# Moving the decay tables of a delta rule from the opening gates of a mixer to its inverse

## The chip, the cores and the metric

The kernel runs on one core of one Trainium2 chip. The metric is the device time of one execution in microseconds, the median of several runs; smaller is better. The core has a matrix engine (TensorE, in the rows PE for products and PEld for loading their weights), two engines that do most of the elementwise work (VectorE, DVE, and ScalarE, ACT), GpSimd (POOL), and queues that start transfers (mainly SP's). Each engine works through its own instructions in the order in which they were written out for it, and waits on semaphores for the others.

## What is computed

The reference is a first block (a mixer and a mixture of experts), followed by a second block of two layers. Each layer is a mixer of three branches and a feed-forward network. The change lies in the first branch of the mixer, a gated delta rule over chunks of 64 places:

```python
g = -jnp.exp(a_log) * jax.nn.softplus(a + dt_bias)
G = jnp.cumsum(gate_chunks(g), axis=-1)
decay = jnp.exp(jnp.where(causal, G[..., :, None] - G[..., None, :], -jnp.inf))
kk = jnp.einsum('bhnck,bhnsk->bhncs', k, k)
M = jnp.where(strict, beta[..., :, None] * kk * decay, 0.0)
T = lax.linalg.triangular_solve(eye + M, ...)          # the inverse
qk = jnp.einsum('bhnck,bhnsk->bhncs', q, k) * decay
q_dec = q * jnp.exp(G)[..., None]
g_last = jnp.exp(G[..., -1])
```

The other two branches are a sparse attention and a gated recurrence (HGRN). Queries, keys and values of the delta rule go through a short convolution and a SiLU first. There are 256 tokens, 1024 channels and 4 heads of 128.

## The kernel before

Everything is in float32; a dense projection is made exact enough by splitting both operands into a high and a low part and adding three products. `dense` (L193) does one 1024 by 256 projection: it loads the weights, and for each half of them `split` (L173) makes the high part `whi` with a cast on ScalarE and the low part `wlo` with a subtraction on VectorE; TensorE then does 24 products per half, 48 in all, into one PSUM bank. There are two buffers each of `whi` and `wlo`, so the cast for a half has to wait until TensorE is through with the half two before it. The bank is one of two that all dense projections of a mixer take turns with, and it comes free when the projection has been read out of it.

A mixer (L1458) opens with the step "gates": small projections, the gates of the delta rule (`delta_gates`, L1568), and the first part of the HGRN gates ("cf"). In `delta_gates` the running sums G of the decays are made, and from them the two tables of 128 by 512 per token half t: `E`, the exponential of minus the distance between two places' sums (four Abs activations that read a PSUM bank with a bias per head, and one Exp), and `eG`, the exponential of the sum itself. `dgl` is the last column of each chunk. On ScalarE these are 4 + 1 + 1 activations per token half and two small copies. `E` is first read in `delta_inverse` (L1645, making `N`), and `eG` near the end of the branch.

Then come the steps in the order of `emit` (L1181): k0 and k1 (the two halves of the key projection), qi, bq, sp0, ci, inv, v1, and so on. k0 and k1 are read out by `conv` (L1445): per block of 128 channels a scaled copy on ScalarE (L1449), in the second block also a copy `raw` (L1452), and three multiply-adds on VectorE (L1456); `silu2` follows (L1560). The step "inv" forms the keys' Gram matrix, `N`, and a blockwise inverse in six levels. "hg" is the HGRN.

What stands when on each engine is set by a list scheduler at build time: each step has a priority from its place in `order` (L1180), where an earlier place is more urgent among the instructions that the scheduler holds to be ready ("gates" is place 0, "inv" comes after both key halves, qi, bq, sp0 and ci); `issue_after(x)` keeps an instruction behind x on its engine. The same code runs for both layers, so the program has two mixers of this kind; in the trace before, the first opens at about 867 us and the second at about 1288 us.

Of the kernel before, what the change touches and what calls it, by code (L numbers as in the profile page):

```python
# [13 lines left out]
AF = mybir.ActivationFunctionType  # L14
# [3 lines left out]
P = 128  # L18
# [46 lines left out]
class K:  # L65
# [106 lines left out]

    def split(self, hi, lo, src):  # L173

        self.nc.scalar.copy(hi, src)  # L175
        with self.tc.issue_after(self.normed0) if self.normed0 else contextlib.nullcontext():
            self.nc.vector.tensor_sub(lo, src, hi.bitcast(F32))  # L177

# [1279 lines left out]
    def mixer(self, l, mp, hh, hl, hu, rb):  # L1458
        nc, v = self.nc, self.v2[l]
# [6 lines left out]
        T = lambda name, shape, dt=F32, tag=None, bufs=1: mp.tile([P, *shape], dt, name=name, tag=tag or name, bufs=bufs)  # L1466
# [18 lines left out]
        with self.level("gates"):  # L1485
            self.dense32(wb(), wv, [(2312, P), (2696, 68), (2048, 8)], hu, ev, blocks=((0, P), (P, 76)))

            ps = self.bk("delta")
# [8 lines left out]
            ps = self.bk("delta")  # L1497
# [5 lines left out]
            gt = self.delta_gates(T, v, baN)  # L1503
# [9 lines left out]
        qkv = [T("dqkv", (4, S), tag="d4", bufs=N_D4) for _ in range(3)]  # L1513

        def load(n, u):
            def ev(a):
                for b in range(2):
                    c = 2 * u + b
                    self.conv(qkv[n][:, c, :], a[:, b, :],
                              [v["conv"][:, k, 4 * n + c:4 * n + c + 1] for k in range(4)],  # L1520
                              T("raw", (S,), bufs=2) if b else None)
                x = qkv[n][:, 2 * u:2 * u + 2, :]
                self.silu2(T, x, x)
            self.dense(wv, [(512 * n + 256 * u, 256)], X, ev)
        oh, ol = (self.big(n, other) for n in ("oh", "ol"))
        sz, sg = T("sz", (2, 512)), T("sg", (2, S))
        qi, bq, cq, ci = (T(n, (2, S)) for n in ("qi", "bq", "cq", "ci"))
        dn = {}

        def z(n):  # L1530
            self.dense(wv, [(1536 + 256 * n, 256)], X,
                       lambda a: self.silu2(T, sz[:, :, n * S:(n + 1) * S], a), tokens=True)
        steps = dict(
            k=lambda n: load(1, n), v=lambda n: load(2, n), q=lambda n: load(0, n), z=z,
            inv=lambda: dn.update(self.delta_inverse(T, qkv[1], gt)),
            rest=lambda: self.delta_rest(T, qkv, gt, dn),
            chunks=lambda: self.delta_chunks(T, v, dn, sz, oh, ol),

# [29 lines left out]
    def delta_gates(self, T, v, baN):  # L1568
        nc, V = self.nc, self.nc.vector
        hv = lambda a: a.rearrange("p (h c) -> p h c", h=4)  # L1570
        bt, ga, gb = T("bt", (2, 4)), T("ga", (2, 4)), T("gb", (2, 4))
        V.tensor_tensor(ga, baN[:, :, 4:], v["dt"][:, None, :].to_broadcast([P, 2, 4]), op=OP.add)
        nc.scalar.activation(gb, ga, AF.Abs)
        with self.tc.issue_after(self.gelu) if self.gelu else contextlib.nullcontext():
            self.table = nc.scalar.preload_act_table_set("natural_log_exp_and_others").ins
            with self.tc.issue_after(self.table):
                nc.scalar.activation(gb, gb, AF.Exp, scale=-1.0)
        nc.scalar.activation(gb, gb, AF.Ln, bias=1.0)
        V.scalar_tensor_tensor(ga, ga, 0.0, gb, op0=OP.max, op1=OP.add)
        V.scalar_tensor_tensor(ga, ga, -1.0, v["a"][:, None, :].to_broadcast([P, 2, 4]), op0=OP.mult, op1=OP.mult)  # L1580
        nc.scalar.activation(bt, baN[:, :, :4], AF.Exp, scale=-1.0)
        V.tensor_scalar(bt, bt, 1.0, None, op0=OP.add)
        V.reciprocal(bt, bt)

        ps = self.bk("delta")
        g2 = ga.rearrange("p t h -> p (t h)")
        nc.tensor.matmul(ps[:, :8], self.c("tri"), g2, start=True, stop=True, skip_group_check=True)
        nc.tensor.matmul(ps[:, 8:16], self.c("bones"), g2, start=True, stop=True, skip_group_check=True)
        G, nG, eg, ed = T("G", (8,)), T("nG", (8,)), T("eg", (2, 4)), T("ed", (2, 4))
        V.tensor_copy(G, ps[:, :8])  # L1590
        V.tensor_scalar(nG, G, -1.0, None, op0=OP.mult)
        nc.scalar.activation(eg.rearrange("p t h -> p (t h)"), ps[:, :8], AF.Exp)
        V.tensor_tensor(ed.rearrange("p t h -> p (t h)"), ps[:, 8:16], G, op=OP.subtract)
        nc.scalar.activation(ed, ed, AF.Exp)

        eG, E = T("eG", (2, 4, P), tag="d4", bufs=N_D4), T("E", (2, 4, P), tag="d4", bufs=N_D4)
        for t in range(2):
            ps = self.bk("delta")
            for h in range(4):
                nc.tensor.matmul(ps[:, h * P:(h + 1) * P], ga[:, t, h:h + 1].to_broadcast([P, P]), self.c("tri"),  # L1600
                                 start=True, stop=True, skip_group_check=True)
            for h in range(4):
                k = 4 * t + h
                nc.scalar.activation(E[:, t, h, :], ps[:, h * P:(h + 1) * P], AF.Abs, bias=nG[:, k:k + 1])
            nc.scalar.activation(E[:, t], E[:, t], AF.Exp, scale=-1.0)
            nc.scalar.activation(eG[:, t], hv(ps), AF.Exp)
        gl = T("dgl", (4, 4))
        for t in range(2):
            nc.scalar.copy(gl[:, 2 * t:2 * t + 2, :], eG[:, t, :, 63:P:64].rearrange("p h n -> p n h"))
        return dict(bt=bt, eg=eg, ed=ed, eG=eG, E=E, gl=gl)  # L1610

    def sumsq(self, T, x):

# [383 lines left out]
```

## Time and profile before

| | |
|---|---|
| time, median of 3 runs | 1686.42 us (1682.34 to 1689.22) |
| the profiled execution, its own time | 1691.02 us |
| its span, first to last instruction | 1689.2 us |
| TensorE busy | 1615.7 us, 96% |
| VectorE busy | 919.5 us, 54% |
| ScalarE busy | 639.2 us, 38% |
| mean granted TensorE clock | 0.983 of full |

The profile's page gives shares over the whole span. What a change in one place does is read from the timeline and the waits of that place: which engine ended a wait of TensorE there, and what that engine was doing just before. A granted clock of 1.00 is the level of 2.4 GHz, 0.50 that of 1.2 GHz; a mean between them over a stretch tells how much of it was spent at each.

### The profile page before, as it was taken

How to read it: one execution, taken by the hardware profiler on the slowest of the kernel's cores; microseconds unless marked ns; L12 is line 12 of the kernel's file. 1: busy time of each engine (PE TensorE's matmuls, PEld its weight loads, DVE VectorE, ACT ScalarE, POOL GpSimd, SP SyncE). 2: the span in 40 equal slices, each digit the busy share in tenths (PEclk: the TensorE clock that was granted, in tenths of full speed). 3: DMA queues.
4: the chain of work that ended last, by engine and by line, in shares of the span. 5: the costliest groups of instructions: out<-in, count | busy, mean ns of one | idle time of the engine just before them, and what ended most of it. 6: DMA issues, size and time to landing. Idle time of an engine off the chain costs nothing.

```text
span 1689.2 us, 25550 instructions
## 1 busy us (share of the span) xinstructions
PE 1615.7 (96%) x10391; PEld 1218.3 (72%) x10391; DVE 919.5 (54%) x1873; ACT 639.2 (38%) x1102; POOL 21.8 (1%) x54
## 2 busy tenths in 40 slices
PE   6999999998999999999989999899999999989997
PEld 4778788973444344333478888799988988789986
DVE  2665445661212121121275597778847779778865
ACT  3543233441111011011164353455645545355643
POOL 1000000200000000000000000000000000000000
PEclk9999999998999999999998999999999999999999
DMA  8634545896999999999932142455762322435553
GB/s 310 212 107 127 198 152 161 267 397 272 421 420 421 421 420 420 421 420 421 378 112 75 32 144 76 150 174 178 231 212 64 106 65 90 150 114 192 181 188 137
DMA packets 162201, 381.72 MB, mean 226 GB/s; under 512 B 14180, under 2 KB 123308, under 8 KB 135200
## 3 DMA queue, kind: packets, MB, share of 16 engines
q1 hardware_dynamic: 160640, 378.45, 60.9%
q8 instruction: 83, 1.36, 0.3%
q0 software_dynamic: 1008, 1.33, 0.3%
q14 instruction: 38, 0.31, 0.1%
q10 hardware_dynamic: 432, 0.27, 0.1%
HBM read 378.98 MB, written 1.05 MB: 225 GB/s over the span
## 4 chain that ended last, share of the span: by engine, by line
PE 63%; DVE 7%; ACT 4%; DMA 2%; issue 1%; DVEq 0%; ACTq 0%
PE bk L186 56%; DVE wlo L177 1%; DMA w<-in_ffn_w_down 1%; ACT whi L175 1%; PE bk L1326 1%; PE bk L1666 1%; PE bk L1679 1%; PE bk L1677 1%; PE bk L1078 1%; ACT pscr L151 1%; DMA mw<-in_moe_w 1%; DVE xg L1273 0%; PE bk L1620 0%; DVE x L1266 0%; PE bk L1283 0%
## 5 line engine op out<-in xcount | busy, mean ns | idle before, releaser
L177 DVE TENSOR_TENSOR wlo<-w,whi 128x1024 fp32r<-128x1024 f32 x236 | 287.7, 1222 | 197.2 <-ACT whi L175 186.8
L175 ACT CAST whi<-w 128x1024 fp32r<-128x1024 f32 x236 | 246.2, 1048 | 298.7 <-PE bk L186 264.1
L186 PE MATMUL bk<-hh,whi 128*128 128x256 f32 x960 | 277.2, 289 | 14.8 <-ACT whi L175 8.1
L186 PE MATMUL bk<-hh,wlo 128*128 128x256 f32 x960 | 277.2, 289 | 6.7 <-DVE wlo L177 6.7
L186 PE MATMUL bk<-hl,whi 128*128 128x256 f32 x960 | 275.3, 287 | 0.0
L186 PEld LDWEIGHTS bk<-hh,whi 128*128 128x128 f32 x960 | 187.8, 196 | 17.8 <-ACT whi L175 9.0
L186 PEld LDWEIGHTS bk<-hh,wlo 128*128 128x128 f32 x960 | 187.9, 196 | 9.4 <-DVE wlo L177 8.1
L186 PEld LDWEIGHTS bk<-hl,whi 128*128 128x128 f32 x960 | 187.7, 196 | 0.4
L186 PE MATMUL bk<-w,xg 128*64 128x512 f32 x584 | 156.1, 594 | 2.8 <-ACT xg L1045 2.8
L1068 DVE TENSOR_TENSOR whi<-whi,bk 128x512 f32<-128x512 f32 x16 | 11.0, 687 | 237.9 <-PE bk L186 210.5
L186 PEld LDWEIGHTS bk<-w,xg 128*64 128x64 f32 x584 | 49.3, 137 | 87.6 <-issue 83.2
L186 PE MATMUL bk<-mw,xg 128*64 128x512 f32 x376 | 99.5, 594 | 1.5 <-ACT xg L1045 1.5
L186 PE MATMUL bk<-w,whi 128*64 128x512 f32 x296 | 95.5, 598 | 0.0
L1456 DVE SCALAR_TENSOR_TENSOR cv<-bk,fc,cv 128x255 f32<-128x255 f32 (+1 forms) x160 | 76.6, 479 | 2.8
L186 PEld LDWEIGHTS bk<-mw,xg 128*64 128x64 f32 x376 | 31.7, 137 | 52.4 <-issue 48.9
L186 PE MATMUL bk<-ah,whi 128*128 128x256 f32 x224 | 65.0, 290 | 2.6 <-ACT whi L175 2.6
L186 PE MATMUL bk<-whi,ah 128*128 128x256 f32 x224 | 64.1, 288 | 0.0
L186 PE MATMUL bk<-al,whi 128*128 128x256 f32 x224 | 64.1, 286 | 0.0
L186 PE MATMUL bk<-wlo,ah 128*128 128x256 f32 x224 | 64.0, 286 | 0.0
L186 PE MATMUL bk<-ah,wlo 128*128 128x256 f32 x224 | 63.9, 287 | 0.0
L186 PE MATMUL bk<-whi,al 128*128 128x256 f32 x224 | 63.4, 284 | 0.0
L1326 PE MATMUL bk<-hu,w 128*128 128x128 f32 (+1 forms) x512 | 60.5, 275 | 0.0
(567 smaller groups left out, 3124.3 us busy)
## 6 DMA issues: line engine op xcount, KB each, us to landing
w<-in_moe_w SPq DMA_DIRECT2D x110, 1024.0 KB, 19.8
mw<-in_moe_w SPq DMA_DIRECT2D x66, 1024.0 KB, 19.8
w<-in_w_in SPq DMA_DIRECT2D x50, 1024.0 KB, 5.7
w<-in_ffn_w_up SPq DMA_DIRECT2D x44, 1024.0 KB, 5.3
w<-in_w_mod SPq DMA_DIRECT2D x24, 1024.0 KB, 5.3
w<-in_ffn_w_down SPq DMA_DIRECT2D x22, 1024.0 KB, 4.9
x<-in_moe_w SPq DMA_DIRECT2D x10, 1024.0 KB, 19.8
w<-in_w_out SPq DMA_DIRECT2D x8, 1024.0 KB, 4.8
```

What stands on the lines that cost most here:

```text
L151: self.nc.scalar.activation(scr[:, :x.shape[-1]], x, AF.Square, accum_out=out)
L175: self.nc.scalar.copy(hi, src)
L177: self.nc.vector.tensor_sub(lo, src, hi.bitcast(F32))
L186: return self.nc.tensor.matmul(out, l, r, start=start, stop=stop, skip_group_check=True)
L1068: V.tensor_tensor(hid, hid, h[1], op=OP.mult)
L1078: nc.tensor.transpose(ps[:, j * P:(j + 1) * P], sh[:, :512].rearrange("s (p j) -> s j p", j=4)[:, j, :], self.c("ident"))
L1326: self.nc.tensor.matmul(a[:m, n * S + t * P:n * S + (t + 1) * P], w[:, k, s0:s0 + m], X[:, k, ts], start=k == 0, stop=k == KJ - 1, skip_gr ...
L1456: eng.scalar_tensor_tensor(out[:, d:], ps[:, :S - d], taps[k], out[:, d:], op0=OP.mult, op1=OP.add)
L1666: nc.tensor.matmul(ps[:, h * P:(h + 1) * P], N[:, t, h, :], U[:, t, h, :], start=True, stop=True, skip_group_check=True)
L1677: nc.tensor.matmul(pt[:, h * P:(h + 1) * P], Z[:, h, :], Ti[:, t, h, :], start=True, stop=True, skip_group_check=True)
L1679: nc.tensor.matmul(pu[:, h * P:(h + 1) * P], Ti[:, t, h, :], Z[:, h, :], start=True, stop=True, skip_group_check=True)
```

## The change

`delta_gates` ends with the small vectors; the tables `E`, `eG` and `dgl` move into a new function `delta_decays`, which the step "inv" calls before `delta_inverse`. Each Abs activation is kept behind the last cast of the weights of k1 (`k_split`), which `split` now remembers. No instruction is added or dropped on TensorE, VectorE or ScalarE, and the transfers stand in the same order.

```diff
     def split(self, hi, lo, src):
-        self.nc.scalar.copy(hi, src)
+        self.last_split = self.nc.scalar.copy(hi, src).ins
...
             self.dense(wv, [(512 * n + 256 * u, 256)], X, ev)
+            if n == 1:
+                self.k_split = self.last_split
...
-            inv=lambda: dn.update(self.delta_inverse(T, qkv[1], gt)),
+            inv=lambda: (self.delta_decays(T, gt), dn.update(self.delta_inverse(T, qkv[1], gt))),
...
         nc.scalar.activation(ed, ed, AF.Exp)
+        return dict(bt=bt, eg=eg, ed=ed, ga=ga, nG=nG)
+
+    def delta_decays(self, T, gt):
+        nc = self.nc
+        hv = lambda a: a.rearrange("p (h c) -> p h c", h=4)
+        ga, nG = gt["ga"], gt["nG"]
         eG, E = T("eG", (2, 4, P), tag="d4", bufs=N_D4), T("E", (2, 4, P), tag="d4", bufs=N_D4)
         for t in range(2):
...
-                nc.scalar.activation(E[:, t, h, :], ps[:, h * P:(h + 1) * P], AF.Abs, bias=nG[:, k:k + 1])
+                with self.tc.issue_after(self.k_split):
+                    nc.scalar.activation(E[:, t, h, :], ps[:, h * P:(h + 1) * P], AF.Abs, bias=nG[:, k:k + 1])
...
-        return dict(bt=bt, eg=eg, ed=ed, eG=eG, E=E, gl=gl)
+        gt.update(eG=eG, E=E, gl=gl)
```

With the other priorities the scheduler writes out a different order for the whole mixer. Three places follow, all in the first mixer (in the second the order is the same but for a few rows).

ScalarE before, at the opening: the tables, then the HGRN gates (`cf`), the first read-out of k0 (`dqkv` from the bank) and the two casts of k1's weights.

```order
L1604 ACTIVATE E<-bk_6348,nG 128x128 x4
L1606 ACTIVATE eG<-bk_6348 128x512
L1605 ACTIVATE E<-E 128x512
L1604 ACTIVATE E<-bk_6359,nG 128x128 x4
L1606 ACTIVATE eG<-bk_6359 128x512
L1605 ACTIVATE E<-E 128x512
L1609 COPY dgl<-eG 128x8 x2
L1866 ACTIVATE cf<-cf 128x512
L1449 ACTIVATE dqkv<-bk_6434,col_4569 128x256
L1867 ACTIVATE cf<-cf 128x512
L175 CAST whi<-w 128x1024 x2
```

ScalarE after, where the tables now stand: behind both casts of k1's weights and the first read-out of k0, and ahead of the casts of qi's (the last row). `hd` and `hk` belong to the HGRN, and `raw` is the copy that ends the read-out of k0's bank.

```order
L1614 ACTIVATE E<-bk_6798,nG 128x128 x4
L1616 ACTIVATE eG<-bk_6798 128x512
L1924 ACTIVATE hd<-hd 128x512
L1615 ACTIVATE E<-E 128x512
L1925 ACTIVATE hk_7940<-hd 128x512
L1614 ACTIVATE E<-bk_6809,nG 128x128 x4
L1616 ACTIVATE eG<-bk_6809 128x512
L1615 ACTIVATE E<-E 128x512
L1619 COPY dgl<-eG 128x8 x2
L1449 ACTIVATE dqkv<-bk_6407,col_4569 128x256
L1452 COPY raw<-bk_6407 128x256
L175 CAST whi<-w 128x1024 x2
```

The tables have moved from ahead of k1's casts to between the two read-outs of k0, ahead of qi's casts.

TensorE before, where it makes the sums that the tables read (L1600), inside the products of k0:

```order
L186 MATMUL bk_6434<-hh,whi 128x256
L186 MATMUL bk_6434<-hl,whi 128x256
L1587 MATMUL bk_6334<-ga,cst 128x8
L1588 MATMUL bk_6334<-ga,cst_6253 128x8
L1600 MATMUL bk_6348<-cst,ga 128x128 x4
L1600 MATMUL bk_6359<-cst,ga 128x128 x4
L186 MATMUL bk_6434<-hh,wlo 128x256
```

TensorE after, the same place:

```order
L186 MATMUL bk_6407<-hh,whi 128x256
L186 MATMUL bk_6407<-hl,whi 128x256
L1589 MATMUL bk_6334<-ga,cst 128x8
L1590 MATMUL bk_6334<-ga,cst_6253 128x8
L1609 MATMUL bk_6798<-cst,ga 128x128 x4
L1609 MATMUL bk_6809<-cst,ga 128x128 x4
L186 MATMUL bk_6407<-hh,wlo 128x256
```

Here nothing moved: only ScalarE's part of the tables comes later.

VectorE before, where the first value projection v1 is read out (`dqkv` from bank 7059), about the middle of the inverse (`Ti` and `U` are its two matrices; bank 6943 is of its third level):

```order
L177 TENSOR_TENSOR wlo<-w,whi 128x1024
L1456 SCALAR_TENSOR_TENSOR dqkv<-bk_7059,col_4569,dqkv 128x255
L1658 COPY_PREDICATED Ti<-cst_6253,bk_6943 128x64x4
L1456 SCALAR_TENSOR_TENSOR dqkv<-bk_7059,col_4569,dqkv 128x254
L1658 COPY_PREDICATED U<-cst_6253,bk_6944 128x64x4
L1456 SCALAR_TENSOR_TENSOR dqkv<-bk_7059,col_4569,dqkv 128x253
```

VectorE after, the same read-out (`ssc` are scores of the sparse attention):

```order
L177 TENSOR_TENSOR wlo<-w,whi 128x1024
L1668 COPY_PREDICATED U<-cst_6253,bk_7038 128x8x32
L177 TENSOR_TENSOR wlo<-w,whi 128x1024
L1456 SCALAR_TENSOR_TENSOR dqkv<-bk_7059,col_4569,dqkv 128x255
L1668 COPY_PREDICATED U<-cst_6253,bk_7051 128x8x32
L1456 SCALAR_TENSOR_TENSOR dqkv<-bk_7059,col_4569,dqkv 128x254
L1836 SCALAR_TENSOR_TENSOR ssc<-rl,wi,ssc 128x256
L1456 SCALAR_TENSOR_TENSOR dqkv<-bk_7059,col_4569,dqkv 128x253
```

The read-out of v1 has moved from the middle of the inverse to its last level.

## Rows read from the trace of the kernel before

**Rows 1.** The page: busy time, share and instructions of each engine.

```profile
PE 1615.7 (96%) x10391; PEld 1218.3 (72%) x10391; DVE 919.5 (54%) x1873; ACT 639.2 (38%) x1102; POOL 21.8 (1%) x54
```

**Rows 2.** Busy time by stretch, with the granted clock (PEclk); two mixers.

```profile
core 0: us, PE busy (x) PEld busy (x) DVE busy (x) ACT busy (x) POOL busy (x), PEclk, DMA share, GB/s
879.50:890.00 10.50, 6.90 (x35) 6.51 (x34) 9.07 (x16) 6.83 (x12) 0.00 (x0) 0.67 0.00 0
902.00:912.00 10.00, 10.00 (x73) 9.99 (x72) 4.17 (x13) 5.70 (x9) 0.00 (x0) 0.83 0.33 106
912.00:923.00 11.00, 11.00 (x47) 9.34 (x46) 7.90 (x28) 2.46 (x6) 0.00 (x0) 0.54 0.09 25
980.00:1020.00 40.00, 38.06 (x326) 35.95 (x327) 37.16 (x65) 22.83 (x43) 0.00 (x0) 1.00 0.37 118
1300.00:1310.00 10.00, 8.73 (x69) 8.12 (x68) 8.61 (x14) 7.73 (x13) 0.00 (x0) 1.00 0.32 96
```

**Rows 3.** TensorE's waits, 868 to 930 us, first mixer: total us, times, longest.

```profile
PE bk L186 <- DVE wlo L177: 2.6, 2, 1.6
PE bk L186 <- ACT whi L175: 2.0, 1, 2.0
PE bk L186 <- ACT qi L1539: 1.5, 1, 1.5
```

**Rows 4.** TensorE's waits, 1288 to 1330 us, second mixer.

```profile
PE bk L1642 <- DVE dqkv L1566: 0.9, 1, 0.9
PE bk L186 <- DVE wlo L177: 0.8, 1, 0.8
PE bk L186 <- ACT whi L175: 0.3, 1, 0.3
PE bk L186 <- ACT raw L1452: 0.2, 1, 0.2
```

**Rows 5.** ScalarE's timeline, first mixer: start us, us, line, operation [idle before].

```profile
874.42 1.12 ACT L1604 ACTIVATE E<-bk,nG 128x128 f32<-128x128 f32 x4
...
878.61 0.70 ACT L1866 ACTIVATE cf<-cf 128x512 f32<-128x512 f32 x1
879.56 0.47 ACT L1449 ACTIVATE dqkv<-bk,col 128x256 f32<-128x256 f32 x1 [0.25 <-PE bk L186]
...
880.45 1.98 ACT L175 CAST whi<-w 128x1024 fp32r<-128x1024 f32 x2
...
882.87 0.46 ACT L1449 ACTIVATE dqkv<-bk,col 128x256 f32<-128x256 f32 x1
883.23 0.36 ACT L1452 COPY raw<-bk 128x256 f32<-128x256 f32 x1
...
885.71 0.63 ACT L1910 ACTIVATE hq<-hd 128x512 f32<-128x512 f32 x1 [0.76 <-DVE hd L1908]
886.25 0.61 ACT L1911 ACTIVATE hk<-hd 128x512 f32<-128x512 f32 x1
```

**Rows 6.** VectorE's timeline, first mixer.

```profile
880.07 0.48 DVE L1456 SCALAR_TENSOR_TENSOR dqkv<-bk,col,dqkv 128x255 f32<-128x255 f32 x1 [6.17 <-ACT dqkv L1449]
...
882.36 1.22 DVE L177 TENSOR_TENSOR wlo<-w,whi 128x1024 fp32r<-128x1024 f32 x1
```

**Rows 7.** TensorE's timeline, first mixer, from k0 to k1.

```profile
879.13 0.28 PE L186 MATMUL bk<-hl,whi 128*128 128x256 f32 x1
879.25 0.28 PE L186 MATMUL bk<-hh,wlo 128*128 128x256 f32 x1
881.54 0.39 PE L186 MATMUL bk<-hh,whi 128*128 128x256 f32 x1 [2.02 <-ACT whi L175]
...
883.63 0.58 PE L186 MATMUL bk<-hh,wlo 128*128 128x256 f32 x1 [1.58 <-DVE wlo L177]
```

## The prediction, made before the changed kernel ran

> **What bounds the kernel now.** I read the page first: TensorE is busy for 1615.7 us of a span of 1689.2 us [rows 1]. Work that no engine is added to or spared can therefore move the time in only two ways, by the 73.5 us in which TensorE is idle and by the clock at which it works. Then I looked for the two mixers, since the change touches nothing else, and asked for busy time by stretch and TensorE's waits around their openings. In the first mixer TensorE is busy for only 6.90 of 10.50 us right after k0, at a mean granted clock of 0.67; the clock is again below 1.00 from 902 to 912 and from 912 to 923 us [rows 2]. Its three waits there are 2.0 us for a cast, 2.6 us in two waits for a low part, and 1.5 us for the copy of qi, 6.1 us together [rows 3]. In the second mixer, with the same program, the waits come to 2.2 us [rows 4] and the clock stays at 1.00 [rows 2]. So the first opening has about 6 us of idle time and some of half clock to give, and the second hardly anything.
>
> Why TensorE waits after k0 is in ScalarE's timeline. The tables run from 874.42 to 878.61, 4.2 us; behind them stand a piece of the HGRN gates, the first read-out of k0, which can't start before k0 is done, and only then the casts of k1's weights, at 880.45 [rows 5]. k0's last product starts at 879.25, k1's first at 881.54, and the stream goes on from 883.63 [rows 7]. That is the stall that the change goes at.
>
> **The change, part by part.** All is reckoned from the profiled execution, whose own time is 1691.02 us (1.8 us beyond its span); it lies 4.6 us above the median of 1686.42 us, and I carry the difference over to the median at the end. No instruction is added, so there is no new work to price; the transfers keep their order, and the first loads that depend on a freed buffer (for ci) are let go earlier than before, not later. On TensorE the products for the tables stay where they are, so they cost what they did. They hold two of the three banks of the delta rule some 9 us longer; the next to want one is the key norm's sum, which takes the third, so I put this at nothing.
>
> First, what goes. k1's casts no longer stand behind the tables and k0's read-out. The first half's cast needs k0's first 24 products done. Products start every 0.12 us [rows 7], so that is 24 x 0.12 = 2.9 us before k0's end at 879.25 + 0.28 = 879.53: at 876.65. The second half's cast can start at 879.5. With 1.0 us for a cast (1.98 for two [rows 5]) and 1.22 for a low part [rows 6], both are there before TensorE wants them, and k1's 48 products follow k0's without a gap. The idle 2.02 + 1.58 us after k0 goes. The two later waits (1.0 and 1.5 us) also hang on late casts and read-outs of k1 and qi, and by the new order k1 is read out in one go, so I let them go too: 6.1 us. In the second mixer the same steps free 2.2 us.
>
> Second, what comes. The tables are still 4.2 us of ScalarE time, and now they stand ahead of `raw` and of qi's casts; that is the wait the change adds. ScalarE's first HGRN activation after the casts needs a result of VectorE that comes 3.35 us after the start of the first low part (882.36 to 885.71 [rows 5, 6]); with the low part started at 877.65 it runs at 881.0. From there to qi's casts ScalarE has: four HGRN activations at 0.54 (885.71 to 886.25), 2.16; two read-outs at 0.36 (882.87 to 883.23), 0.72; the tables, 4.19; `raw`, 0.36: 7.4 us [rows 5]. qi's first cast starts at 888.4. TensorE's first product came 1.09 us after its cast started (880.45 to 881.54), and the first with a low part 1.27 us after the subtraction started (882.36 to 883.63) [rows 5 to 7]; so 889.5 and, with the subtraction right behind the cast, 890.7. k1's 48 products end at 879.25 + 48 x 0.12 + 0.28 = 885.3. TensorE is idle for 4.2 us, does two products, and waits 0.7 us more: a **new stall of 4.9 us between k1 and qi**. Counted from the end of k0, every term is the same in the second mixer, so it comes there too. The nearest row that shows a stall of this kind is the old one of 3.6 us; that is my lower end, 4.9 the upper and my value, since it follows from rows of the very instructions.
>
> Third, the clock. After the 3.6 us of idle time the first mixer ran below full clock: 0.67 over 10.5 us is 6.9 us at the lower level [rows 2]. Of those, between 6.9 and 6.9 - 4.1 = 2.8 us (883.63 - 879.53 = 4.1) were spent on products, which costs half of it, 1.4 to 3.5; I take 2.4. The stretch from 902 to 912 gives 0.34 x 10 / 2 = 1.7 us, behind the waits of 1.0 and 1.5 us. Both go with their stalls; but the new stall is longer than the one that brought the first, so I set 2.4 us for it in both mixers. The second mixer's 1.1 us of waits at the same place left the clock at 1.00 [rows 2, 4], so an opening without a long stall can hope for full clock. The page "TensorE: Matmul & The Clock Gate" of the Trainium skill (HAM oscillation) says that a wait in a stream of products brings the clock down and that each restart begins slow. By that rule the two charges of 2.4 us are due; were it not so here, the sum would be 4.8 us lower. The stretch from 912 to 923 us, at 0.54, costs 0.46 x 11 = 5.1 us; I see no stall ahead of it, so I leave it as it is.
>
> The sum: first mixer -6.1 - 2.4 - 1.7 + 4.9 + 2.4 = -2.9 us; second mixer -2.2 + 4.9 + 2.4 = +5.1 us. **Net +2.2 us**: 1693.2 us for the profiled execution, 1688.6 us against the median. The rest of the mixers' order changes too, but their products are the same and TensorE is busy for 38 of 40 us there [rows 2]; I put that at nothing, with 3 us either way.
>
> **The rivals.** *The clock repays it.* The slow stretch at 912 us does not recur, since in the second mixer the same steps ran at 1.00, and the new stalls leave the clock alone: 2.2 - 5.1 - 4.8 = -7.7 us, 1678.7 us. For it: the order puts 29 dense products behind the key norm's sum, where before there were few. Against it: the new stall is longer than the old. With stalls of 3.6 us instead of 4.9 it is -10.3 us, 1676.1 us. The page's rule named above speaks against the second half of this rival.
>
> *VectorE's full stretch.* The read-out of v1 moves from the middle of the inverse to its end, so two low parts at 1.22 and six multiply-adds at 0.48 [rows 6], 5.3 us with nothing for the SiLU, land ahead of the stretch from 980 to 1020, where VectorE is busy for 37.16 of 40 us and has 2.8 us to spare [rows 2]. If TensorE's remaining products all wait on VectorE there, each mixer loses 5.3 - 2.8 = 2.5 us, and with the tables' stall in both openings 2.2 + 5.0 = +7.2 us, 1693.6 us. If the slow clock of 912 us comes in the second mixer as well, 5.1 more: 1698.7 us. It decides from the point at which TensorE has no dense products left while VectorE is behind.
>
> *The stall is covered.* If the scheduler's order lets qi's casts in no later than k1's end, only the gains stay: -10.2 - 2.2 = -12.4 us, 1674.0 us. The order speaks against it: the tables and `raw` stand ahead of qi's casts in both mixers.
>
> **How the numbers follow.** Forecast 0.58, the clock rival 0.20, VectorE's 0.17, the covered stall 0.05. The likeliest time is 1688.6 us. The range leaves out the covered stall and the far ends of two rivals: 1678.5 to 1697 us. A measurement of this kernel can tell about 0.5%, 8.4 us, from no change: faster means under 1678.0, slower over 1694.8. Faster gets the covered stall and a third of the clock rival, 0.11; slower gets most of VectorE's rival and the forecast's upper edge, 0.17; within 0.5% the rest, 0.72.
>
> **What would show it.** In the profile after: no wait of TensorE between k0 and k1 in either mixer; ScalarE's casts for k1 ahead of the tables; a wait of 4 to 5 us of TensorE on ScalarE's cast or `raw` at the start of qi, in both mixers, with a granted clock near 0.67 behind it; the stretch after the key norm's sum at half clock or not, by which the first rival is told. The prediction is wrong if qi's products follow k1's without such a gap, if the clock stays at 1.00 across it, or if the gap that decides lies later, where VectorE is full.

## The result: 0.9% slower, and the profile after

The changed kernel takes 1703.84 us (median of four runs, 1702.04 to 1707.03) against 1687.59 us: a ratio of 1.0094 with a 95% interval of 1.0072 to 1.0116. A second comparison, run e12 below, gave 1.0069 (1.0043 to 1.0094). So the change costs 12 to 16 us; the forecast was +2.2 us, with 1697 us as its upper end. The profiled execution took 1702.47 us (span 1700.7) against 1691.02 us.

The page's first part (compare [rows 1]) shows TensorE busy for 8 us longer with the same 10391 instructions:

```profile
PE 1623.7 (95%) x10391; PEld 1227.1 (72%) x10391; DVE 921.9 (54%) x1873; ACT 639.7 (38%) x1102; POOL 21.8 (1%) x54
```

A busy TensorE that does the same work for longer is either at a lower clock or does it in pieces that run less closely. Busy time by stretch (columns as in [rows 2]) shows the clock:

```profile
884.00:896.00 12.00, 7.49 (x39) 6.99 (x39) 7.06 (x12) 8.62 (x20) 0.00 (x0) 0.72 0.27 85
902.00:912.00 10.00, 9.54 (x81) 8.52 (x80) 8.96 (x27) 6.65 (x12) 0.00 (x0) 1.00 0.34 106
912.00:923.00 11.00, 10.71 (x89) 10.19 (x90) 10.38 (x42) 2.00 (x5) 0.00 (x0) 1.00 0.30 97
955.00:965.00 10.00, 7.86 (x54) 7.66 (x53) 7.99 (x24) 4.19 (x6) 0.00 (x0) 0.83 0.34 105
1014.00:1026.00 12.00, 12.00 (x84) 10.35 (x82) 7.76 (x26) 1.33 (x3) 0.00 (x0) 0.66 0.27 89
...
1310.00:1320.00 10.00, 8.26 (x43) 7.86 (x44) 7.32 (x13) 6.24 (x9) 0.00 (x0) 0.66 0.34 105
...
1380.00:1390.00 10.00, 7.87 (x53) 7.87 (x54) 7.95 (x21) 3.55 (x5) 0.00 (x0) 0.83 0.34 105
```

In the first mixer the slow stretches at 902 to 923 us are gone, and others have come: behind a wait at 884 to 888 us, at 960 us, and from 1018 us on, where TensorE had no wait at all (busy for 12.00 of 12 us in the row from 1014). The second mixer, which had run at 1.00 throughout, has two of them. TensorE's waits at the two openings (868 to 930 us, then 1288 to 1340 us; compare [rows 3, 4]; `Z` and `Ti` belong to the inverse):

```profile
PE bk L186 <- ACT whi L175: 4.1, 1, 4.1
PE bk L186 <- DVE wlo L177: 0.8, 2, 0.5
PE bk L1687 <- ACT Z L1683: 0.8, 1, 0.8
PE bk L1687 <- DVE Ti L1668: 0.2, 1, 0.2
```

```profile
PE bk L186 <- ACT whi L175: 4.1, 1, 4.1
PE bk L186 <- DVE wlo L177: 1.1, 2, 0.8
```

TensorE's timeline says where the 4.1 us lie: between k1's last product, at 884.19, and qi's first, with k1 right behind k0 and no wait between them.

```profile
884.19 0.28 PE L186 MATMUL bk<-hh,wlo 128*128 128x256 f32 x1
888.52 0.58 PE L186 MATMUL bk<-hh,whi 128*128 128x256 f32 x1 [4.05 <-ACT whi L175]
...
889.78 0.58 PE L186 MATMUL bk<-hh,wlo 128*128 128x256 f32 x1 [0.46 <-DVE wlo L177]
```

ScalarE's timeline shows what stands ahead of qi's casts (compare [rows 5]): the tables from 881.47 on, then the read-out of k0.

```profile
881.47 1.14 ACT L1614 ACTIVATE E<-bk,nG 128x128 f32<-128x128 f32 x4
...
886.51 0.37 ACT L1619 COPY dgl<-eG 128x8 f32<-128x8 f32 x2
886.71 0.55 ACT L1449 ACTIVATE dqkv<-bk,col 128x256 f32<-128x256 f32 x1
887.08 0.44 ACT L1452 COPY raw<-bk 128x256 f32<-128x256 f32 x1
887.33 2.08 ACT L175 CAST whi<-w 128x1024 fp32r<-128x1024 f32 x2
```

So the opening is as forecast. What was not forecast comes later. Each mixer can be cut into three parts: the idle time before TensorE's products, the time lost to the clock (one minus the granted clock, times the length, summed over stretches of 5 us), and the rest. From the first transpose of the opening to the first product behind the mixer, in the two profiles:

| | first mixer before | after | second mixer before | after |
|---|---|---|---|---|
| length, us | 204.6 | 206.1 | 192.4 | 202.9 |
| idle | 11.8 | 11.3 | 7.9 | 11.6 |
| lost to the clock | 10.2 | 10.2 | 0.0 | 5.1 |
| the rest | 182.6 | 184.6 | 184.5 | 186.3 |

These are one execution of each kernel; in the profile of e12 the same changed mixers took 200.8 and 206.0 us, and nearly all of that difference is time lost to the clock (5.1 and 8.5 us). Where the clock falls during a wait, that time stands in both rows, 0.7 us of it in the first mixer before. Outside the mixers the two profiles agree within a microsecond in each of the three parts (ahead of the first mixer, between the two, behind the second). Over all runs of a comparison, whose clocks are recorded too, the time lost to the clock (by each run's mean clock) is 32.8 and 31.2 us for the changed kernel (two comparisons) and 24.4 to 26.7 us for the kernel before; the time without it is 1671 against 1663.5 us. The loss is thus about half clock and half waits and slower work.

**The place that was missed.** In the later half of each mixer TensorE waits for the copy that reads out ci's bank. TensorE's row there, of before and then of after:

```profile
967.81 0.39 PE L186 MATMUL bk<-hh,whi 128*128 128x256 f32 x1 [1.62 <-ACT ci L1546]
```

```profile
959.32 0.39 PE L186 MATMUL bk<-hh,whi 128*128 128x256 f32 x1 [2.14 <-ACT ci L1548]
```

And ScalarE's timeline ahead of it, of before and of after:

```profile
966.23 1.04 ACT L175 CAST whi<-w 128x1024 fp32r<-128x1024 f32 x1 [0.17 <-PE bk L186]
967.18 0.58 ACT L1546 COPY ci<-bk 128x512 f32<-128x512 f32 x1
```

```profile
957.22 1.04 ACT L175 CAST whi<-w 128x1024 fp32r<-128x1024 f32 x1 [0.96 <-PE bk L186]
958.17 0.62 ACT L1567 ACTIVATE th<-dqkv 128x512 f32<-128x512 f32 x1
958.70 0.57 ACT L1548 COPY ci<-bk 128x512 f32<-128x512 f32 x1
```

The read-out of v1 had moved from the middle of the inverse to its end, and v1's SiLU with it: its tanh (`th`) now stands between a cast and ci's copy. TensorE waits 2.14 us in place of 1.62, in both mixers, and behind it the clock falls (0.83 from 955 to 965 and from 1380 to 1390 us, above). Before, the same stretch ran at full clock:

```profile
963.00:975.00 12.00, 10.38 (x82) 9.67 (x81) 11.26 (x31) 5.04 (x8) 0.00 (x0) 1.00 0.29 89
```

### The profile page after: what moved, and what is told of

It reads as the page before. It is cut to its first block, busy times and chain, and to the rows that moved or that the text cites. A ratio compares the mean times of both kernels' runs of the same rounds, so it can differ in the third digit from the quotient of the medians.

```text
span 1700.7 us, 25559 instructions
## 1 busy us (share of the span) xinstructions
PE 1623.7 (95%) x10391; PEld 1227.1 (72%) x10391; DVE 921.9 (54%) x1873; ACT 639.7 (38%) x1102; POOL 21.8 (1%) x54
```

## The experiments

All are compared with runs of the kernel before on the same chip.

**One mixer at a time (e1, e2).** In both, the old place is used where `l` isn't in the list, (0,) or (1,):

```diff
             gt = self.delta_gates(T, v, baN)
+            self.k_split = None
+            if l not in (0,):
+                self.delta_decays(T, gt)
...
-            inv=lambda: (self.delta_decays(T, gt), dn.update(self.delta_inverse(T, qkv[1], gt))),
+            inv=lambda: (l in (0,) and self.delta_decays(T, gt), dn.update(self.delta_inverse(T, qkv[1], gt))),
...
```

> The tables move in the first mixer alone; the second is written out as before. Theory A (the two traces' ledger: each mixer pays 3.7 us of idle and 5.1 us of half clock behind the late tables and about 2.2 us of slower small products at its end, and the first mixer alone had as much idle and half clock before, which go): about +1.5 us, between -2 and +5. Theory B (the new place costs both mixers alike, and the first mixer's lost slow stretches have nothing to do with it): about half of the whole, +6 to +8 us.

> The tables move in the second mixer alone. Theory A: about +11 us (1.0065), and with the run above it adds up to the changed kernel's +12 to +16 us. Theory B: +6 to +8 us, as in the first mixer.

Measured: 1.0014 (0.9999 to 1.0028) for the first mixer alone, 1692.37 against 1690.02 us, and 1.0049 (1.0035 to 1.0063) for the second alone, 1699.17 us. That is +2.4 and +9.2 us, together +11.5. Theory A holds, B falls: the same new order costs four times as much in the second mixer, because the first had its own 6.1 us of waits and half clock to give back. The profile of e2 also holds the first mixer in the old order: 200.3 us long, against 204.6 in the profile of before, with the slow stretch at 912 us absent. So that stretch, charged at 5.1 us in the prediction, comes and goes between executions of one and the same order.

**The wait alone (e3).** The tables keep the priority of "gates", behind k1's casts:

```diff
-            inv=lambda: (self.delta_decays(T, gt), dn.update(self.delta_inverse(T, qkv[1], gt))),
+            inv=lambda: (self.early_decays(T, gt), dn.update(self.delta_inverse(T, qkv[1], gt))),
...
+    def early_decays(self, T, gt):
+        with self.level("gates"):
+            self.delta_decays(T, gt)
```

> The tables keep the urgency of the opening gates; only the wait behind k1's second cast is added. TensorE's and VectorE's orders come out word for word as in the changed kernel, and ScalarE's differs by two HGRN activations per mixer. Theory A (what costs is where the tables stand on ScalarE, ahead of qi's casts): the same time as the changed kernel, +12 to +16 us. Theory C (the step's lower urgency is what costs): clearly less, 0 to +5 us.

Measured: 1.0067 (1.0048 to 1.0086), the changed kernel's time. Theory C falls. So the step's other priority, by which the section on the change explains the new order, is not what re-orders the mixer. The written-out orders of programs that were not run go further: without the wait, but with the step still called in "inv", they are word for word those of the changed kernel, and the tables stay late when the step is called right behind k0's with the urgency of "gates". Called with that urgency ahead of k0's step, the orders are those of the kernel before. So it is the place in the code, behind k0's step, that re-orders the mixer. Why the tables can't come ahead of k0's read-out once they are written behind it in the code wasn't settled.

**Behind bq's casts (e4).**

```diff
-            if n == 1:
-                self.k_split = self.last_split
...
-            bq=lambda: self.dense(wv, [(2056, 256)], X, lambda a: nc.scalar.copy(bq, a)),
+            bq=lambda: (self.dense(wv, [(2056, 256)], X, lambda a: nc.scalar.copy(bq, a)), setattr(self, "k_split", self.last_split)),
```

> The tables wait for the second cast of bq's weights instead of k1's, so they stand behind the casts of k1, qi and bq. TensorE's order at the end of the mixers comes out nearly as before the change. Theory A: the stall between k1 and qi (4.5 us in each mixer), the half clock behind it and the slower end all go, while k1's casts stay early: the first mixer gains 8 to 13 us on the kernel before, the second stays within 1 us of it; -8 to -14 us, 1674 to 1680 us. Theory D (tables so late hold up the key's read-out and the inverse instead): a new wait of some 4 us ahead of the inverse, and 0 to +8 us.

Measured: 0.9995 (0.9985 to 1.0006). The stall at qi is gone, but theory D's wait stands in its place, in both mixers; TensorE's waits from 868 to 930 us begin with the keys' Gram products (L1650), which want a bank that the tables still hold:

```profile
PE bk L1650 <- ACT eG L1614: 3.9, 2, 2.6
```

**Half of the tables (e5 to e8).** In e5 the first token half stays in the opening and the second waits for the first of k1's two casts (`splits` is the list of all casts so far); in e6 it waits for the second (`self.splits[-1]`).

```diff
...
             gt = self.delta_gates(T, v, baN)
+            self.delta_decays(T, gt, 0)
...
+            if n == 1 and u == 1:
+                self.k_split = self.splits[-2]
+                with self.level('gates'):
+                    self.delta_decays(T, gt, 1)
...
```

> The first token half's tables stay in the opening, the second half's wait for the first cast of k1's weights and come right behind it. TensorE's order at the mixers' ends stays that of the kernel before. Theory A (the price is 4.2 us of tables in one piece ahead of casts that TensorE is about to need): half of them, 2.1 us, delays k1's casts by less than TensorE's backlog, so the first mixer's 3.6 us wait falls to about 1 us, nothing new appears at qi, and half clock behind k0 goes: -4 to -8 us, 1682 to 1686 us against 1690 of the kernel before in the last comparison. Theory E (ScalarE's delay only moves on to a later read-out or cast, as when the tables waited for bq's casts): waits of the same sum elsewhere, within 2 us of the kernel before.

> As the run above, but the second half's tables wait for the second cast of k1's weights, so both casts go early. Here TensorE's order at the mixers' ends comes out as in the changed kernel (the HGRN's last products ahead of the delta rule's chunk scan). Theory F (that order alone costs 2 us in each mixer): the opening gains 4 to 8 us as above and the ends give 4 us back: -4 to 0 us, 2 to 4 us slower than the run above. Theory G (the ends' order costs nothing, the 2 us belong to the opening's stall): at or below the run above.

Measured: e5 0.9996 (0.9982 to 1.0010), e6 1.0010 (0.9998 to 1.0023). Theory E's time, but for another reason: in e5's profile the first mixer takes 193.1 us, 7 to 11 less than in the old order, and the second 200.2, 8 more. There the key's SiLU now comes later, and the Gram products wait for it (waits of the second opening, 1278 to 1330 us):

```profile
PE bk L1656 <- DVE dqkv L1574: 2.6, 1, 2.6
PE bk L189 <- ACT qi L1547: 1.5, 1, 1.5
PE bk L189 <- DVE wlo L180: 1.1, 2, 0.7
```

e6 is 4 us slower than e5, as theory F had it, but not by slower work: without the clock's part e6's runs take 1661.7 us against 1662.6, and lose 29.1 us to the clock against 24.8. It has one wait of 4.7 to 4.8 us in each opening, for `raw`. But theory F, that the order at the ends has a price of its own, doesn't fall with that, since the clock can be the price. TensorE's late stretch in the first mixer, of e5 and then of e6:

```profile
1010.00:1026.00 16.00, 15.72 (x137) 12.60 (x137) 11.72 (x32) 4.58 (x12) 0.00 (x0) 1.00 0.17 57
```

```profile
1010.00:1026.00 16.00, 15.92 (x137) 13.96 (x137) 10.44 (x38) 4.70 (x10) 0.00 (x0) 0.89 0.37 132
```

In e6 the clock falls there in both mixers, at a cost of 1.7 us each, with TensorE busy for 15.92 of 16 us. All profiles of this case point the same way. Where the HGRN's products (`hq,hk`) stand wholly ahead of the chunk scan, the clock fell between the two in 11 of 18 mixers (in the changed kernel, e1, e6, e7, e9, e10, e11 and e12), by 1.7 to 5.1 us. Where the chunk scan begins before the HGRN is through, as in the kernel before, it fell in that part of 1 mixer of 10 (in e4). In the 11, TensorE had no wait over 0.25 us in the 10 us ahead of the fall; why the clock falls there stays open.

In e7 the whole tables wait for qi's second cast:

```diff
-            if n == 1:
-                self.k_split = self.last_split
...
-            qi=lambda: self.dense(wv, [(2440, 256)], X, lambda a: nc.scalar.copy(qi, a)),
+            qi=lambda: (self.dense(wv, [(2440, 256)], X, lambda a: nc.scalar.copy(qi, a)), setattr(self, "k_split", self.last_split)),
```

> The tables wait for qi's second cast and stand right behind it, ahead of the rest of k0's and k1's read-outs. TensorE's order at the ends is as in the changed kernel. Theory A: no stall between k1 and qi; the 4.2 us come back as a wait at bq, whose bank and casts hang on the read-outs behind the tables, 3 to 5 us in each mixer, with the ends' 2 us each: +5 to +10 us. Theory G: the wait at bq alone, +1 to +5 us.

Measured: 1.0045 (1.0029 to 1.0061), +7.6 us by the means. The wait has moved to bq, as expected, and is longer:

```profile
PE bk L186 <- ACT raw L1452: 5.9, 1, 5.9
```

Its runs lose 31.4 us to the clock against 24.4, and the time without that is 1664.1 against 1663.5 us, as if the whole loss were clock. But the clock here falls while TensorE still waits for `raw`, and what it loses while TensorE is idle costs nothing (the wait ends at 888.38 us):

```profile
885.00:892.00 7.00, 3.62 (x17) 3.62 (x18) 2.44 (x6) 5.21 (x14) 0.00 (x0) 0.51 0.49 150
```

In this profile 3.6 us of the two mixers' 13.6 us of lost clock lie in the two waits, against 0.7 of 10.2 in the profile of before. So the split gives the clock up to some 3 us too much; part of the loss is the waits.

e8 is e5 with the halves in the first mixer only (both halves in the opening where `l` is 1):

> The halved tables of the run e5 in the first mixer alone; the second mixer is written out as before. In e5's profile the first mixer took 193.1 us against 204.6 and 200.3 us in two profiles with the old order, the second 200.2 against 192.4 us. Theory A (each mixer's gain and loss are its own): -6 to -9 us, 1679 to 1682 us, faster than both kernels. Theory H (a mixer's time swings by the clock from run to run, and e5's two mixers show only that): within 2 us of the kernel before.

Measured: **0.9939 (0.9927 to 0.9951), 1679.17 us**: faster than both kernels, and theory A's figure. TensorE's waits from 868 to 930 us are 3.3 us in all, where [rows 3] had 6.1, and none of them is for a cast:

```profile
PE bk L189 <- DVE wlo L180: 1.9, 2, 1.2
PE bk L1659 <- DVE dqkv L1577: 0.9, 1, 0.9
PE bk L189 <- ACT raw L1455: 0.5, 1, 0.5
```

The clock stays at 1.00 from 880 to 900 us, where it was 0.67 behind k0 in [rows 2].

**The wait at ci by itself (e9).** The kernel before, with

```diff
-            ci=lambda: self.dense(wv, [(3276, 256)], X, lambda a: nc.scalar.copy(ci, a), tokens=True),
+            ci=lambda: self.dense(wv, [(3276, 256)], X, lambda a: (nc.scalar.copy(ci, a), nc.scalar.copy(ci, a)), tokens=True),
```

> The kernel before, with ci's read-out made a second time right behind the first (0.53 us more of ScalarE that TensorE waits for). Nothing else is changed in the code; the order that the scheduler writes out behind it moves somewhat. Theory I (a wait of 1.6 us leaves the clock alone there and one of 2.1 us brings it down, as between the two traces): the wait at ci grows to about 2.1 us in both mixers, the granted clock falls behind it, and the time grows by 1.1 us of waits and 1.7 to 3.4 us of half clock in each mixer: +4 to +8 us. Theory J (the clock there has nothing to do with the wait's length): +1 us, and a clock of 1.00 behind ci.

Measured: 0.9976 (0.9957 to 0.9994), faster, so the time settles nothing; the order behind ci moved more than "somewhat". (The ten runs spread from 1678.9 to 1691.9 us.) The place itself does tell: the wait is 2.24 us in both mixers, and the clock behind it fell in the first and not in the second:

```profile
955.00:965.00 10.00, 7.76 (x50) 7.20 (x48) 8.36 (x26) 4.26 (x6) 0.00 (x0) 0.83 0.34 105
1363.00:1373.00 10.00, 7.76 (x62) 7.20 (x61) 9.48 (x27) 4.25 (x6) 0.00 (x0) 1.00 0.34 105
```

In the profiles of this case the wait at ci was 1.62 us ten times (before, e1, e2, e4, e5 and e8 with the mixers in those orders), and the clock behind it never fell; it was 2.1 to 2.2 us fourteen times, and the clock fell ten times, in all seven of the first mixer and three of the second. Theory I holds as a chance, not as a rule. The gain of e9 lies elsewhere, at the start of the feed-forward networks, where the wait for a cast fell from 2.89 to 1.43 us and the clock no longer dropped. The stretch of before, and the one of e9:

```profile
1092.00:1102.00 10.00, 7.68 (x40) 7.48 (x41) 6.28 (x9) 3.87 (x5) 0.00 (x0) 0.66 0.64 209
```

```profile
1088.00:1098.00 10.00, 9.95 (x83) 9.95 (x84) 7.53 (x12) 4.84 (x7) 0.00 (x0) 1.00 0.56 187
```

**Thinner tables (e10).** Changed kernel, with

```diff
-            for h in range(4):
-                k = 4 * t + h
-                with self.tc.issue_after(self.k_split):
-                    nc.scalar.activation(E[:, t, h, :], ps[:, h * P:(h + 1) * P], AF.Abs, bias=nG[:, k:k + 1])
+            with self.tc.issue_after(self.k_split):
+                nc.scalar.activation(E[:, t], hv(ps), AF.Abs, bias=nG[:, 4 * t:4 * t + 1])
...
-            nc.scalar.activation(eG[:, t], hv(ps), AF.Exp)
+        eG = E
```

> The changed kernel with the tables' work on ScalarE cut to about half in the same place: one Abs per token half with one bias for all four heads in place of four, and no second table (the first is read in its place), so the tables hold wrong numbers; everything else is computed as before. The tables take some 2.3 us instead of 4.2. Theory A: the wait between k1 and qi falls from 4.5 to about 2.6 us in both mixers, 3.8 us in all, and the half clock behind it stays or shrinks with it: 4 to 8 us less than the changed kernel, +4 to +9 us against the kernel before. Theory K (the wait is set by something else that is late there, such as the HGRN's activations or k0's read-out): under 1 us less than the changed kernel, +11 to +16 us.

Measured: 1.0050 (1.0028 to 1.0072), 1696.6 us, +8.2 us against the kernel before on its chip, where e12 had +15.0 on another. The two intervals overlap, so the times alone don't decide; the wait does. The wait at qi shrinks by what the tables shrink; TensorE's waits from 868 to 935 us, first two rows:

```profile
PE bk L186 <- ACT whi L175: 2.2, 1, 2.2
PE bk L186 <- DVE wlo L177: 1.0, 2, 0.8
```

and the clock behind it recovers in part in the first mixer and wholly in the second:

```profile
890.00:905.00 15.00, 12.08 (x85) 11.49 (x84) 10.84 (x18) 10.42 (x22) 0.00 (x0) 0.89 0.23 71
1305.00:1320.00 15.00, 12.08 (x98) 11.49 (x97) 11.65 (x20) 11.64 (x23) 0.00 (x0) 1.00 0.46 141
```

Theory A holds, K falls: the tables took 2.4 us of ScalarE's timeline in place of 4.2, and the wait fell by as much, from 4.1 to 2.2 us in both mixers. The tables' own length sets the stall.

**Both gains together (e11), and the changed kernel again (e12).** e11 has the edits of e8 and e9.

> The halved tables in the first mixer alone (run e8, 0.9939) and ci's read-out made twice (run e9, 0.9976) together; the orders are those of the two runs side by side. Theory A (the effects lie in different places, e8's in the first opening, e9's at the starts of the feed-forward networks, and each is the wait and the half clock behind it): 0.9939 x 0.9976 = 0.9915, 1672 to 1676 us. Theory H (the clock takes back what the waits give): no better than e8 alone, 1679 to 1682 us.

> The changed kernel once more beside the same runs of the kernel before, since four runs gave +16 us and the sum by mixers (runs e1 and e2) +11.5 us. Theory A (the mixers add up): 1.006 to 1.008, +10 to +13 us. Otherwise there is something that only both mixers together cost: 1.009 or more.

Measured: e11 0.9936 (0.9915 to 0.9957), 1679.16 us, no better than e8. Its feed-forward networks keep e9's gain (210.6 us between the mixers, against 215.7 in e8), and its mixers lose as much: 196.5 and 197.8 us against 193.1 and 192.5, with 3.4 us each lost to the clock where e8 lost 1.7 and nothing. Theory A falls. H has the right time, but of the 8.7 us that the mixers give back the clock is 5.1; the rest is slower work. e12 gave 1.0069, +15.0 us by the medians; with +11.5 for e1 and e2 that is within the intervals, so nothing is shown that only both mixers together cost.

## Why the prediction was wrong, step by step

- **k1 right behind k0: right**, in both mixers. k1's casts stand ahead of the tables, and no wait is left between the halves.
- **A new stall between k1 and qi: right in place and size.** Forecast 4.9 us (4.2 and 0.7); measured 4.05 + 0.46 = 4.5 us in the first mixer and 4.06 + 0.76 = 4.8 in the second. e10 shows that the tables' own length sets it: with 1.8 us less of them its first wait was 1.9 us shorter.
- **The waits of the first opening: a little off.** I let 6.1 us go and 4.9 come; 5.9 us stand there after, since 0.8 and 0.2 us appear at the inverse. In the second it is 5.2 us against the forecast 4.9, and the same two at the inverse follow just behind the rows shown, at 1342 and 1347 us.
- **The clock at the openings: about right.** For the first mixer I let 4.1 us go and charged 2.4. By the rows, 0.33 x 10.5 + 1.7 = 5.2 us went and (1 - 0.72) x 12 = 3.4 came, with nothing more up to 923 us: 1.8 us gained, where I had 1.7. In the second mixer it is 0.34 x 10 = 3.4 where I set 2.4. The Trainium skill's page "TensorE: Matmul & The Clock Gate" (HAM oscillation), weighed in the prediction, agrees with the two openings here, at granted clocks of 0.72 and 0.66; e10's second mixer, with a wait of 2.2 us and a clock of 1.00, shows that not every wait does it.
- **The stretch at 912 us: charged to one execution.** I left its 5.1 us in place; e2 shows it gone in the unchanged order, and the first rival's gain of 5.1 us was of this kind too. The profile of after doesn't have it, but loses as much from 1018 us on, in the stretch between the HGRN and the chunk scan that the new order brings (see e6). That the sums agree, 10.2 us lost before and after, is luck.
- **"The rest of the mixers' order changes too ... I put that at nothing": the step that failed.** Its reason was that the products are the same and TensorE was busy for 38 of 40 us. But the row that it rests on, 980 to 1020 us, doesn't hold the wait at ci (967.81 before), and v1's SiLU came to stand ahead of ci's read-out. That is 0.5 us of wait and, in the profile of after, 1.7 us of half clock in each mixer. And the prediction knew only two ways to lose time, idle time and the clock; a third is that the same small products run less closely, about 2 us in each mixer (the row "the rest" above). Together that is some 4 us a mixer, 8 us, beside the +2.2 forecast: 10.6 us. The late half clock between the HGRN and the chunk scan adds, over the ten profiled mixers whose end is in the changed kernel's order, 1.5 us a mixer on average (15.3 us in four of them): 13.6 us, where e1 and e2 gave 11.5 and the two comparisons 12 to 16. The 3 us set for either side were too few. These shares are read from the profiles; no run takes one of them away alone.
- **The rival that came nearest**, VectorE's full stretch, had the right cause, v1's read-out at the inverse's end, but priced it on the wrong engine: VectorE's work was the same, and ScalarE's 0.53 us ahead of one copy counted. Its +7.2 us were short as well.

Of the 2 us in small products a part can be shown. The eighty products of the HGRN's levels take, from each one's start to the next product's, 6.56 us before, 7.83 after and 6.44 in e6 and e7. A first group of sixteen took 1.09 us before (1417.26 to 1418.35), and after 1.64 us where products of the sparse attention (`PT,vN`) stand between two such groups (1426.00 to 1427.64). Before, then after:

```profile
1417.26 1.16 PE L186 MATMUL bk<-hq,hk 64*128 64x128 f32 x16
1418.35 1.16 PE L1717 MATMUL bk<-dqkv 128*128 128x128 f32 x8
```

```profile
1426.00 1.71 PE L186 MATMUL bk<-hq,hk 64*128 64x128 f32 x16
1427.64 0.65 PE L1863 MATMUL bk<-PT,vN 128*64 128x256 f32 x2
1428.22 1.71 PE L186 MATMUL bk<-hq,hk 64*128 64x128 f32 x16
```

But before, too, a group of sixteen took 1.70 us (1419.94 to 1421.64), with other neighbours, so the neighbours shown are no sure cause. What slows these products stays open, as does the remainder of the 2 us.

## What to carry to other kernels

Where a list scheduler writes out the order, an edit at the opening of a stage can re-order the whole stage: go through the reads of each bank that the matrix engine waits for, down to the end, and ask what now stands ahead of each on the reading engine. Here work of 4 us in one piece only moved its stall to the next cast behind it (k1, qi, bq or the inverse, in turn); cut in two, with a cast between, it fitted into the first mixer's opening for a gain of 0.6%. And the same code in two layers need not want the same order: the split that gained 7 us or more in the first mixer lost 8 us in the second. Last, a time lost to the clock that is reckoned from a run's mean clock also counts what was lost during waits; look where the clock fell before you call a loss clock.

## What the runs showed of the hardware that was not expected

- The granted clock has its own spread: one and the same order of a mixer took 200.3 us and 204.6 us in two executions, by a half-clock stretch of 5.1 us that stood in one and not in the other. A stretch at half clock seen in one profile is no sure charge.
- At one place a slightly longer wait brought the clock down. Waits of 1.62 us ahead of ci left the clock at 1.00 in ten of ten places; 2.1 to 2.2 us brought it down in ten of fourteen; the 4.1 us between k1 and qi brought it down in both openings of the profile of after. No threshold was measured, and at another place, the opening of e10's second mixer, a wait of 2.2 us left the clock at 1.00.
- The clock also fell with no wait to speak of ahead of it: in the profile of after from 1018 us on, with TensorE busy for 12.00 of 12 us at a mean clock of 0.66. That part of the mixer had it in 11 of 18 mixers where the HGRN stands ahead of the chunk scan, and in 1 of 10 where the two overlap.
